# Attention scores on TensorE: the low parts of each head padded to 128 rows

## The chip, the core and the metric

The kernel runs on one core of one Trainium2 chip. A core has five engines that run side by side and meet at semaphores: TensorE (PE; its weight loads are listed apart as PEld), VectorE (DVE), ScalarE (ACT), GpSimd (POOL) and SyncE (SP, which here issues the transfers). The metric is the device time of one execution in microseconds (us), lower is better. A run is timed several times, and one execution is also recorded by the hardware profiler.

## The reference

One activation of 512 tokens by 1024 channels goes through two blocks of two layers each. Three of the mixers hold attention scores, and those are what the change touches:

```
# mLSTM, 8 heads of 64 (chunked in the reference):
s = einsum('bhtd,bhsd->bhts', qt, kt) * exp(dmat - m_t)
# causal attention with forget bias, 16 heads of 64:
logits = einsum('bqhd,bkhd->bhqk', qi, k) + (ci - c)
# neighbourhood attention, 8 heads of 64, plus 256 context keys:
s_loc = einsum('brqhd,brkwhd->bhrqkw', qg, k_band) * scale + bias
s_ctx = einsum('brqhd,bchd->bhrqc',  qg, k_ctx)  * scale
```

All inputs are float32, and every head has 64 dimensions, so a score product contracts over 64.

## The kernel before, in words

Features lie on the 128 partitions, tokens along the free dimension. To keep float32 accuracy with single-pass matmuls, each operand is split in two: a high part (the value rounded to the matmul format, written by ACT) and a low part (the rest, by DVE). A projection then takes three matmuls per block of 128 (`mm3`, L182 to L184, or L241 to L243 with the roles turned): high by high, high by low, low by high.

The kernel runs in eight stages, s0 to s7, one after another; names in the profile begin with the stage. s0 is the mLSTM mixer (`mlstm`), s2 the causal attention (`fox`), s4 the neighbourhood attention (`even_mixer`); s1, s3, s5 and s7 are feed-forward layers, s6 a convolution.

Scores are made for two heads at a time, since two heads of 64 fill the 128 partitions. `left` (L781) makes one tile per head: in the head's own 64 rows the high part, in the other 64 rows the low part. `right` (L787) makes three tiles: for each head a tile that holds the high part twice (L792 writes the copy, L799 the original), and a third tile that holds the low parts of both heads, each in its own 64 rows (DVE, L801). `dots` (L806) then makes the scores of both heads in two passes. The first pass (L809) runs over all 128 rows and sums high by high and low by high in one matmul. The second pass (L812) runs over the head's own 64 rows only, high by low. Per stage there are 32, 64 and 64 second-pass matmuls, 160 in all, with 128 to 512 columns.

`right` is called 18 times: 4 times in s0, 8 times in s2 (two pairs ahead of use), 6 times in s4 (4 pairs of heads, 2 tiles of context keys). Its tiles come from a pool of 53 slots that most tensors of the kernel share; a slot is handed on when its last reader is done.

Order: the program is written stage by stage, but a scheduler orders the instructions of each engine, and so places projection matmuls between those of the scores. Each engine then runs its own list strictly in that order. What stands around the change: in s2, POOL masks the diagonal blocks of the bias rows that DVE adds to the scores (L866, `affine_select`, four per head), in s0 it masks the decay tiles (L640), in s4 it takes square roots (L248). After the scores, DVE and ACT make the softmax (L878 to L891 in s2, L1116 to L1121 in s4), PE turns the probabilities over (L902, L1131) and multiplies by the values (L914, L1141, L1148). Score results lie in four PSUM banks ("aux").

Of the kernel before, what the change touches and what calls it, by code (L numbers as in the profile page):

```python
# [9 lines left out]
F32 = mybir.dt.float32  # L10
F32R = mybir.dt.float32r
AF = mybir.ActivationFunctionType
# [40 lines left out]
HALF = (slice(0, T // 2), slice(T // 2, T))  # L53
# [289 lines left out]
class Normed:  # L343
# [7 lines left out]
    def put(self, k, s, tmp=None):  # L351
        e = self.e
        self.tmp[k, s.start] = tmp
        if self.h[k] is None:
            self.h[k] = e.pair()
        hi, lo = self.h[k]
        return e.split(self.x[k][:, s], hi[:, s], lo[:, s], e.vec(self.w[0], self.w[1] + k))
# [216 lines left out]
def mlstm(e, A, x, first, pre, nxt, extra):  # L574
# [53 lines left out]
    def scores(j):  # L628
        a, b = left(e, kk[j]), right(e, q[j])
        both = e.triangles("dt")  # L630
        mbs = e.wide()
        for i in range(2):
            hd = 2 * j + i
            mb = mbs[:, i * T:(i + 1) * T]
            nc.sync.dma_start(out=mb, in_=md[hd:hd + 1, :].to_broadcast([P, T]))
            for sb in range(NT):
                d = both[i][sb]
                nc.scalar.activation(out=d, in_=mb[:, sb * P:], func=AF.Exp, scale=-1.0,
                                     bias=aT[:, sb * H + hd:sb * H + hd + 1])
                nc.gpsimd.affine_select(out=d[:, :P], in_=d[:, :P], pattern=[[1, P]], base=0, channel_multiplier=-1,  # L640
                                        compare_op=ALU.is_ge, fill=0.0)
        for sbs in ((0,), (1, 3), (2,)):
            ps = [e.bank("aux") for _ in range(2)]
            o = 0
            for sb in sbs:
                n = T - sb * P
                dots(e, [p[:, o:o + n] for p in ps], a, slice(sb * P, (sb + 1) * P), b, slice(sb * P, T))
                o += n
            for i in range(2):
                d = both[i][sbs[0]]  # L650
                if len(sbs) > 1:
                    d = both[i]["1,3"]
                nc.vector.tensor_tensor(out=d, in0=ps[i][:, :o], in1=d, op=ALU.mult)
        return both
# [116 lines left out]
ROWS2 = (slice(0, 64), slice(64, 128))  # L771
# [14 lines left out]

def right(e, t, scale=None, get=same, put=same, out=None):  # L787

    out = out or [e.slot(F32R, name="right") for _ in range(3)]
    for i, r in enumerate(ROWS2):  # L790
        a = out[i]
        e.nc.scalar.activation(out=put(a[ROWS2[1 - i]]), in_=get(t[r]), func=AF.Copy, scale=scale or 1.0)  # L792
        high_low(e, get(t[r]), put(a[r]), put(a[r].bitcast(F32)), put(out[2][r]), scale)
    return out


def high_low(e, src, hi, hi32, lo, scale):
    nc = e.nc
    nc.scalar.activation(out=hi, in_=src, func=AF.Copy, scale=scale or 1.0)  # L799
    if scale is None:  # L800
        nc.vector.tensor_tensor(out=lo, in0=src, in1=hi32, op=ALU.subtract)  # L801
    else:
        nc.vector.scalar_tensor_tensor(out=lo, in0=src, scalar=scale, in1=hi32, op0=ALU.mult, op1=ALU.subtract)


def dots(e, ps, a, acols, b, bcols):  # L806

    for i in range(2):
        e.nc.tensor.matmul(ps[i], lhsT=a[i][:, acols], rhs=b[i][:, bcols], start=True, stop=False)  # L809
    for i in range(2):  # L810
        r = ROWS2[i]
        e.nc.tensor.matmul(ps[i], lhsT=a[i][r, acols], rhs=b[2][r, bcols], start=False, stop=True)  # L812


def fox(e, A, x, wk, pre, nxt):
# [40 lines left out]
    def scores(j):  # L856
# [14 lines left out]
        for qt in range(NT):  # L871
            n = (qt + 1) * P
            ps = [e.bank("aux")[:, :n] for _ in range(2)]
            dots(e, ps, a, slice(qt * P, n), b, slice(0, n))
            for i in range(2):
                p = pr[i][3 - qt]
                m = e.small(5, "mx")
                nc.vector.tensor_tensor_reduce(out=p[:, qt * P:n], in0=ps[i][:, qt * P:n],  # L878
                                               in1=diag[i][:, qt * P:n], op0=ALU.add, op1=ALU.max, scale=1.0,
                                               scalar=NEG, accum_out=m[:, 0:1])  # L880
                if qt:
                    nc.vector.tensor_tensor_reduce(out=p[:, :qt * P], in0=ps[i][:, :qt * P],
                                                   in1=bias[i][:, :qt * P], op0=ALU.add, op1=ALU.max, scale=1.0,
                                                   scalar=NEG, accum_out=m[:, 1:2])
                    nc.vector.tensor_scalar(out=m[:, 2:3], in0=m[:, 0:1], scalar1=m[:, 1:2], scalar2=-1.0,
                                            op0=ALU.max, op1=ALU.mult)
                else:
                    nc.vector.tensor_scalar(out=m[:, 2:3], in0=m[:, 0:1], scalar1=-1.0, scalar2=None, op0=ALU.mult)
                nc.scalar.activation(out=p, in_=p, func=AF.Exp, bias=m[:, 2:3], accum_out=m[:, 3:4])
                nc.vector.reciprocal(m[:, 4:5], m[:, 3:4])  # L890
                nc.vector.tensor_scalar(out=p, in0=p, scalar1=m[:, 4:5], scalar2=None, op0=ALU.mult)  # L891
# [27 lines left out]
    raw, os = [], []  # L919
    queries(1)  # L920
    sides = {0: right(e, kk[0]), 1: right(e, kk[1])}
    pr, th = scores(0), gate()
    for j in range(KT):
        if j + 1 < KT:
            queries(1)
        after = (scores(j + 1), gate()) if j + 1 < KT else None
        if j + 2 < KT:
            sides[j + 2] = right(e, kk[j + 2])
        if j == KT - 2:
            os = [e.split_new(t, 0.5) for t in raw]  # L930
        raw.append(values(j, pr, th))
        if after:
            pr, th = after
        if os:
            os.append(e.split_new(raw[j], 0.5))
# [72 lines left out]
def even_mixer(e, A, x, first, pre, nxt):  # L1008
# [16 lines left out]
    kt, kc = [], []  # L1025
# [9 lines left out]
    for side, n in ((hc, 2), (h, NT)):  # L1035
        for j in range(n):
            t = e.slot(name="v")
# [6 lines left out]
    wqk = Weights(e, A["mix_w_qk"])  # L1044
    project(1)
    for t in kt:
        three = right(e, t)
        kc += [[c[:, s] for c in three] for s in HALF]
    v = {}
    for c in (0, 16, 8, 24, 40, 32, 48):  # L1050
        v[c] = e.slot(name="vw")
# [44 lines left out]
    def scores(j, half):  # L1096
        if half == 0:
            biases[j] = []
            for i in range(2):
                t = e.wide()  # L1100
                nc.sync.dma_start(out=t, in_=A["rpb"][2 * j + i])
                biases[j].append(t)
        pr = [[e.slot(name="p") for _ in range(2)] for _ in range(2)]
        for z in range(2):
            qt = half * 2 + z
            k0, which = WINDOWS[qt][0] * ROWS, (0, 1, 1, 2)[qt]
            ps = [e.bank("aux") for _ in range(2)]
            a, own = q[j], kk[j]
            for b, cols, d in ((own, slice(k0, k0 + 256), HALF[0]), (kc[j], HALF[0], HALF[1])):
                dots(e, [p[:, d] for p in ps], a, slice(qt * P, (qt + 1) * P), b, cols)  # L1110
            for i in range(2):
                p, b, s = pr[i][z], biases[j][i], e.small(4, "sm")
                b = bass.AP(tensor=b.tensor, offset=b[:, which * 256:].offset,
                            ap=[list(b.ap[0]), [768 - 256 * which, 2], [1, 256]])
                two = "p (a b) -> p a b"
                nc.vector.tensor_tensor_reduce(out=p.rearrange(two, a=2), in0=ps[i].rearrange(two, a=2), in1=b,  # L1116
                                               op0=ALU.add, op1=ALU.max, scale=1.0, scalar=NEG, accum_out=s[:, 0:1])
                nc.vector.tensor_scalar(out=s[:, 1:2], in0=s[:, 0:1], scalar1=-1.0, scalar2=None, op0=ALU.mult)
                nc.scalar.activation(out=p, in_=p, func=AF.Exp, bias=s[:, 1:2], accum_out=s[:, 2:3])
                nc.vector.reciprocal(s[:, 3:4], s[:, 2:3])  # L1120
                nc.vector.tensor_scalar(out=p, in0=p, scalar1=s[:, 3:4], scalar2=None, op0=ALU.mult)  # L1121
        return pr
# [29 lines left out]
    a, b, out = [], [], []  # L1152
    pr = scores(*steps[0])
    spatial_norm()
    for n, (j, half) in enumerate(steps):
# [6 lines left out]
        if n == len(steps) - 1:  # L1162
            out = [e.split_new(t) for t in a]
            out += [e.split_new(t) for t in b]
        values(j, half, pr, po)
        if half == 1:
            t = e.slot(name="b")
# [464 lines left out]
```

## Time and profile before

| | |
|---|---|
| median of 3 runs | 2566.67 us (2564.92 to 2566.76) |
| the profiled execution | 2563.47 us, of which span 2561.7 us |
| PE busy | 2496.2 us, 97% of the span |
| DVE busy | 1598.2 us, 62% |
| ACT busy | 1135.8 us, 44% |
| POOL busy | 76.7 us, 3% |
| mean granted TensorE clock | 0.988 |

Busy times add up how long an engine held instructions. For PE they are modelled ends of pipelined matmuls, so "97% busy" does not say that it ran at its peak: the distance from one matmul's start to the next one's start says how fast they follow each other. Where a row of the timeline merges several equal instructions (x2), its start is that of the first.

### The profile page before, as it was taken

How to read it: one execution, taken by the hardware profiler on the slowest of the kernel's cores; microseconds unless marked ns; L12 is line 12 of the kernel's file. 1: busy time of each engine (PE TensorE's matmuls, PEld its weight loads, DVE VectorE, ACT ScalarE, POOL GpSimd, SP SyncE). 2: the span in 40 equal slices, each digit the busy share in tenths (PEclk: the TensorE clock that was granted, in tenths of full speed). 3: DMA queues.
4: the chain of work that ended last, by engine and by line, in shares of the span. 5: the costliest groups of instructions: out<-in, count | busy, mean ns of one | idle time of the engine just before them, and what ended most of it. 6: DMA issues, size and time to landing. Idle time of an engine off the chain costs nothing.

```text
span 2561.7 us, 33896 instructions
## 1 busy us (share of the span) xinstructions
PE 2496.2 (97%) x12954; PEld 2043.8 (80%) x12954; DVE 1598.2 (62%) x3249; ACT 1135.8 (44%) x1882; POOL 76.7 (3%) x226
## 2 busy tenths in 40 slices
PE   9999999999999999999999999999999999999998
PEld 7778888888776688888887768878889678888887
DVE  7776866676557758576776665837375566634343
ACT  6555534243357645342445653423234765423231
POOL 0110000000001000000000000000000000000000
PEclk9999999999999999999999999999999998999999
DMA  6433243422332322424234223536251320322221
GB/s 214 173 113 124 94 145 110 140 91 76 120 107 83 109 77 99 157 98 164 91 114 134 101 85 112 184 130 237 103 210 64 103 81 32 101 91 99 91 91 34
DMA packets 91475, 293.27 MB, mean 114 GB/s; under 512 B 10008, under 2 KB 16408, under 8 KB 91312
## 3 DMA queue, kind: packets, MB, share of 16 engines
q1 hardware_dynamic: 90080, 290.04, 32.8%
q8 instruction: 102, 1.67, 0.3%
q10 hardware_dynamic: 1232, 1.06, 0.1%
q14 instruction: 61, 0.50, 0.1%
HBM read 283.67 MB, written 7.39 MB: 114 GB/s over the span
## 4 chain that ended last, share of the span: by engine, by line
PE 84%; ACT 5%; DVE 5%; issue 3%; DMA 1%; POOL 1%; POOLq 0%; SPq 0%; DVEq 0%; ACTq 0%
PE s1aux L184 3%; PE s1aux L182 3%; PE s1aux L183 3%; PE s3aux L182 3%; PE s3aux L184 3%; PE s3aux L183 3%; PE s7aux L182 2%; PE s7aux L184 2%; PE s7aux L183 2%; PE s5aux L183 2%; PE s5aux L184 2%; PE s5aux L182 2%; PE s1mm L184 2%; PE s1mm L182 2%; PE s1mm L183 2%
## 5 line engine op out<-in xcount | busy, mean ns | idle before, releaser
L170 DVE TENSOR_TENSOR s7wlo<-s7wst,s7whi 128x1024 fp32r<-128x1024 f32 x60 | 73.5, 1225 | 132.5 <-ACT s7whi L169 122.4
L169 ACT ACTIVATE s5whi<-s5wst 128x1024 fp32r<-128x1024 f32 x64 | 68.0, 1063 | 177.6 <-PE s5aux L183 85.8
L169 ACT ACTIVATE s7whi<-s7wst 128x1024 fp32r<-128x1024 f32 x60 | 63.7, 1062 | 168.0 <-PE s7aux L183 89.2
L170 DVE TENSOR_TENSOR s5wlo<-s5wst,s5whi 128x1024 fp32r<-128x1024 f32 x64 | 78.2, 1224 | 76.5 <-ACT s5whi L169 76.2
L169 ACT ACTIVATE s3whi<-s3wst 128x1024 fp32r<-128x1024 f32 x66 | 70.0, 1061 | 101.0 <-PE s3aux L183 53.6
L169 ACT ACTIVATE s1whi<-s1wst 128x1024 fp32r<-128x1024 f32 x66 | 69.8, 1061 | 97.6 <-PE s1aux L183 46.4
L170 DVE TENSOR_TENSOR s3wlo<-s3wst,s3whi 128x1024 fp32r<-128x1024 f32 x66 | 80.8, 1224 | 33.6 <-ACT s3whi L169 33.3
L170 DVE TENSOR_TENSOR s1wlo<-s1wst,s1whi 128x1024 fp32r<-128x1024 f32 x66 | 80.7, 1223 | 31.7 <-ACT s1whi L169 31.5
L170 DVE TENSOR_TENSOR s2wlo<-s2wst,s2whi 128x1024 fp32r<-128x1024 f32 (+1 forms) x41 | 49.2, 1200 | 57.6 <-ACT s2whi L169 57.4
L182 PE MATMUL s2mm<-s2hh,s2whi 128*128 128x512 f32 (+1 forms) x192 | 73.0, 386 | 2.5 <-ACT s2hh L169 1.3
L183 PE MATMUL s2mm<-s2hl,s2whi 128*128 128x512 f32 (+1 forms) x192 | 73.9, 386 | 0.0
L184 PE MATMUL s2mm<-s2hh,s2wlo 128*128 128x512 f32 (+1 forms) x192 | 73.8, 385 | 0.0
L184 PE MATMUL s1aux<-s0hh,s1wlo 128*128 128x512 f32 x176 | 69.8, 396 | 0.0
L182 PE MATMUL s3aux<-s2hh,s3whi 128*128 128x512 f32 x176 | 69.3, 394 | 0.0
L184 PE MATMUL s3aux<-s2hh,s3wlo 128*128 128x512 f32 x176 | 69.3, 394 | 0.0
L183 PE MATMUL s3aux<-s2hl,s3whi 128*128 128x512 f32 x176 | 69.3, 394 | 0.0
L183 PE MATMUL s1aux<-s0hl,s1whi 128*128 128x512 f32 x176 | 69.2, 393 | 0.0
L182 PE MATMUL s1aux<-s0hh,s1whi 128*128 128x512 f32 x176 | 69.2, 393 | 0.0
L752 DVE SCALAR_TENSOR_TENSOR s1c<-s1u,vecs,s1c 128x511 f32<-128x511 f32 (+1 forms) x88 | 65.2, 748 | 5.0 <-ACT s1c L750 3.6
L169 ACT ACTIVATE s2whi<-s2wst 128x1024 fp32r<-128x1024 f32 (+1 forms) x41 | 42.6, 1041 | 55.0 <-PE s2mm L183 40.4
L752 DVE SCALAR_TENSOR_TENSOR s3c<-s3u,vecs,s3c 128x511 f32<-128x511 f32 (+1 forms) x88 | 64.9, 747 | 2.8 <-ACT s3c L750 1.5
L970 DVE CUSTOM_DVE_ANT_0 s5mj<-s5wm,sc 128x512 f32<-128x512 f32 x96 | 62.4, 688 | 0.3
(732 smaller groups left out, 8077.9 us busy)
## 6 DMA issues: line engine op xcount, KB each, us to landing
s5wst<-w_ff SPq DMA_DIRECT2D x60, 512.0 KB, 3.7
s7wst<-w_ff SPq DMA_DIRECT2D x60, 512.0 KB, 3.2
s5wm<-w_mod SPq DMA_DIRECT2D x48, 512.0 KB, 3.9
s1wst<-ffn_w_up SPq DMA_DIRECT2D x40, 512.0 KB, 3.2
s3wst<-ffn_w_up SPq DMA_DIRECT2D x40, 512.0 KB, 3.2
s1wst<-ffn_w_down SPq DMA_DIRECT2D x22, 512.0 KB, 3.2
s3wst<-ffn_w_down SPq DMA_DIRECT2D x22, 512.0 KB, 3.2
s6wst<-w_pw SPq DMA_DIRECT2D x20, 512.0 KB, 3.3
```

Of the source, the lines that this page charges most:

```text
L169: nc.scalar.activation(out=hi, in_=src, func=AF.Copy)
L170: return nc.vector.tensor_tensor(out=lo, in0=src, in1=hi.bitcast(F32), op=ALU.subtract)
L182: mm(ps, lhsT=w[0], rhs=h[0], start=first, stop=False)
L183: mm(ps, lhsT=w[0], rhs=h[1], start=False, stop=False)
L184: self.last = mm(ps, lhsT=w[1], rhs=h[0], start=False, stop=last)
L752: nc.vector.scalar_tensor_tensor(out=c[:, t:], in0=u[:, :T - t], scalar=w[2 - t], in1=c[:, t:], op0=ALU.mult, op1=ALU.add)
L970: nc.vector.tensor_tensor_reduce(out=junk, in0=w[:, i * T:(i + 1) * T], in1=sc[i], op0=ALU.mult, op1=ALU.add, scale=1.0, scalar=0.0, accum ...
```

## The change

`right` makes four tiles in place of three. The low parts of the two heads lie in tiles of their own; in each, the other 64 rows are set to zero by a memset on POOL. The second pass then runs over all 128 rows: the head's high rows meet its low part, and its low rows meet zeros.

```
-    out = out or [e.slot(F32R, name="right") for _ in range(3)]
+    out = out or [e.slot(F32R, name="right") for _ in range(4)]
     for i, r in enumerate(ROWS2):
-        a = out[i]
-        e.nc.scalar.activation(out=put(a[ROWS2[1 - i]]), in_=get(t[r]), func=AF.Copy, scale=scale or 1.0)
-        high_low(e, get(t[r]), put(a[r]), put(a[r].bitcast(F32)), put(out[2][r]), scale)
+        a, b = out[i], out[2 + i]
+        rest = ROWS2[1 - i]
+        e.nc.gpsimd.memset(b[rest].bitcast(F32), 0.0)
+        e.nc.scalar.activation(out=put(a[rest]), in_=get(t[r]), func=AF.Copy, scale=scale or 1.0)
+        high_low(e, get(t[r]), put(a[r]), put(a[r].bitcast(F32)), put(b[r]), scale)
@@ def dots
     for i in range(2):
-        r = ROWS2[i]
-        e.nc.tensor.matmul(ps[i], lhsT=a[i][r, acols], rhs=b[2][r, bcols], start=False, stop=True)
+        e.nc.tensor.matmul(ps[i], lhsT=a[i][:, acols], rhs=b[2 + i][:, bcols], start=False, stop=True)
@@ def even_mixer
-        three = right(e, t)
-        kc += [[c[:, s] for c in three] for s in HALF]
+        four = right(e, t)
+        kc += [[c[:, s] for c in four] for s in HALF]
```

The first pass is L811 in the changed kernel, the second L813, the memset L793, the mask L867.

PE in s2, the scores of the second pair of heads; `s2aux` are the score banks, `s2right_6357` is the tile with both heads' low parts. Before:

```order
L809 MATMUL s2aux_6579<-s2right_6356,s2left_6540 128x128
L812 MATMUL s2aux_6579<-s2right_6357,s2left_6540 128x128
L809 MATMUL s2aux_6596<-s2right_6355,s2left_6539 128x256
L809 MATMUL s2aux_6597<-s2right_6356,s2left_6540 128x256
L812 MATMUL s2aux_6596<-s2right_6357,s2left_6539 128x256
L812 MATMUL s2aux_6597<-s2right_6357,s2left_6540 128x256
L809 MATMUL s2aux_6616<-s2right_6355,s2left_6539 128x384
L809 MATMUL s2aux_6617<-s2right_6356,s2left_6540 128x384
L812 MATMUL s2aux_6616<-s2right_6357,s2left_6539 128x384
L812 MATMUL s2aux_6617<-s2right_6357,s2left_6540 128x384
```

And now, the same place:

```order
L811 MATMUL s2aux_6597<-s2right_6371,s2left_6558 128x128
L813 MATMUL s2aux_6597<-s2right_6373,s2left_6558 128x128
L811 MATMUL s2aux_6614<-s2right_6370,s2left_6557 128x256
L811 MATMUL s2aux_6615<-s2right_6371,s2left_6558 128x256
L813 MATMUL s2aux_6614<-s2right_6372,s2left_6557 128x256
L813 MATMUL s2aux_6615<-s2right_6373,s2left_6558 128x256
L811 MATMUL s2aux_6634<-s2right_6370,s2left_6557 128x384
L811 MATMUL s2aux_6635<-s2right_6371,s2left_6558 128x384
L813 MATMUL s2aux_6634<-s2right_6372,s2left_6557 128x384
L813 MATMUL s2aux_6635<-s2right_6373,s2left_6558 128x384
```

The order is the same; only the second pass reads a tile of each head's own (6372 and 6373 in place of 6357 twice).

PE in s0, the first scores, where `s0mm` are projection matmuls between them. Before:

```order
L809 MATMUL s0aux_974<-s0right_941,s0left_935 128x512
L183 MATMUL s0mm_1010<-hl_143,s0whi_1006 128x512
L184 MATMUL s0mm_1010<-hh_142,s0wlo_1007 128x512
L182 MATMUL s0mm_1010<-hh_146,s0whi_1006 128x512
L183 MATMUL s0mm_1010<-hl_147,s0whi_1006 128x512
L184 MATMUL s0mm_1010<-hh_146,s0wlo_1007 128x512
L812 MATMUL s0aux_974<-s0right_943,s0left_935 128x512
L182 MATMUL s0mm_1176<-hh_118,s0whi_1172 128x512
L809 MATMUL s0aux_975<-s0right_942,s0left_936 128x512
```

And now:

```order
L811 MATMUL s0aux_977<-s0right_941,s0left_935 128x512
L183 MATMUL s0mm_1182<-hl_143,s0whi_1178 128x512
L184 MATMUL s0mm_1182<-hh_142,s0wlo_1179 128x512
L811 MATMUL s0aux_978<-s0right_942,s0left_936 128x512
L811 MATMUL s0aux_985<-s0right_941,s0left_935 128x384
L811 MATMUL s0aux_986<-s0right_942,s0left_936 128x384
L813 MATMUL s0aux_977<-s0right_943,s0left_935 128x512
L813 MATMUL s0aux_985<-s0right_943,s0left_935 128x384
L811 MATMUL s0aux_985<-s0right_941,s0left_935 128x128
L813 MATMUL s0aux_978<-s0right_944,s0left_936 128x512
```

Four projection matmuls that stood between the first score matmuls now come after them.

POOL in s2, the masks of the bias rows (`s2wm`, one row of four masks per head). Before:

```order
L866 AFFINE_SELECT s2wm_6545<-s2wm_6545 128x128 x4
L866 AFFINE_SELECT s2wm_6559<-s2wm_6559 128x128 x4
L866 AFFINE_SELECT s2wm_6782<-s2wm_6782 128x128 x4
L866 AFFINE_SELECT s2wm_6796<-s2wm_6796 128x128 x4
L866 AFFINE_SELECT s2wm_7019<-s2wm_7019 128x128 x4
```

And now:

```order
L867 AFFINE_SELECT s2wm_6563<-s2wm_6563 128x128 x4
L793 MEMSET s2right_6360 64x512
L793 MEMSET s2right_6361 64x512
L793 MEMSET s2right_6372 64x512
L793 MEMSET s2right_6373 64x512
L867 AFFINE_SELECT s2wm_6577<-s2wm_6577 128x128 x4
L867 AFFINE_SELECT s2wm_6803<-s2wm_6803 128x128 x4
L793 MEMSET s2right_6709 64x512
L793 MEMSET s2right_6710 64x512
L867 AFFINE_SELECT s2wm_6817<-s2wm_6817 128x128 x4
```

From here to the end of the stage two memsets stand between the masks of one head of each pair and those of the other.

## Rows read from the trace of the kernel before

**Rows 1.** The page, share of the chain that ended last by engine.

```profile
PE 84%; ACT 5%; DVE 5%; issue 3%; DMA 1%; POOL 1%; POOLq 0%; SPq 0%; DVEq 0%; ACTq 0%
```

**Rows 2.** Stretches s0, s2, s4: length, then busy PE, PEld, DVE, ACT, POOL; clock; DMA.

```profile
86.00:172.00 86.00, 84.28 (x386) 63.81 (x386) 61.98 (x141) 53.71 (x121) 14.55 (x36) 0.97 0.38 129
740.00:885.00 145.00, 142.58 (x680) 99.02 (x679) 114.03 (x470) 96.44 (x217) 19.96 (x52) 1.00 0.25 82
1385.00:1535.00 150.00, 141.19 (x727) 105.69 (x726) 95.80 (x260) 90.47 (x137) 5.08 (x4) 0.95 0.28 92
```

**Rows 3.** Timeline of PE in s2: start, duration, line, output<-inputs, rows*columns of weights, shape.

```profile
759.53 0.22 PE L809 MATMUL s2aux<-s2right,s2left 128*128 128x128 f32 x1
759.68 0.33 PE L812 MATMUL s2aux<-s2right,s2left 64*128 64x128 f32 x1
...
760.27 0.40 PE L182 MATMUL s2mm<-s2hh,s2whi 128*128 128x512 f32 x1
760.50 0.39 PE L183 MATMUL s2mm<-s2hl,s2whi 128*128 128x512 f32 x1
...
764.52 0.39 PE L809 MATMUL s2aux<-s2right,s2left 128*128 128x512 f32 x1
764.84 0.50 PE L812 MATMUL s2aux<-s2right,s2left 64*128 64x512 f32 x1
765.27 0.50 PE L182 MATMUL s2mm<-s2hh,s2whi 128*128 128x512 f32 x1
765.61 0.39 PE L809 MATMUL s2aux<-s2right,s2left 128*128 128x512 f32 x1
```

**Rows 4.** Timeline of PE in s1, 256 columns, all over 128 rows.

```profile
616.55 0.28 PE L184 MATMUL s1aux<-s1gh,s1wlo 128*128 128x256 f32 x1
616.67 0.28 PE L182 MATMUL s1aux<-s1gh,s1whi 128*128 128x256 f32 x1
```

**Rows 5.** Timeline of PE in s4: four score groups; a low part alone.

```profile
1461.59 0.40 PE L809 MATMUL s4aux<-s4right,s4left 128*128 128x256 f32 x2
1461.91 0.38 PE L812 MATMUL s4aux<-s4right,s4left 64*128 64x256 f32 x2
...
1464.47 0.51 PE L182 MATMUL s4mm<-s3hh,s4whi 128*128 128x512 f32 x1
...
1475.02 0.38 PE L812 MATMUL s4aux<-s4right,s4left 64*128 64x256 f32 x1
```

**Rows 6.** Instructions of L812: durations in ns min/median/max, first and last start, shapes.

```profile
L812 PE MATMUL s2aux<-s2right,s2left x64: 323/409/502, 743.3 to 882.9; 64*128 64x128 f32 x16, 64*128 64x256 f32 x16, 64*128 64x384 f32 x16, 64*128 64x512 f32 x16
L812 PE MATMUL s4aux<-s4right,s4left x64: 276/382/579, 1387.9 to 1531.8; 64*128 64x256 f32 x64
L812 PE MATMUL s0aux<-s0right,s0left x32: 322/381/504, 94.1 to 170.6; 64*128 64x512 f32 x8, 64*128 64x384 f32 x8, 64*128 64x128 f32 x8, 64*128 64x256 f32 x8
```

**Rows 7.** Waits of DVE in s2: who waited for whom, total us, times, longest.

```profile
DVE s2mx L890 <- ACT s2p L889: 8.2, 10, 1.2
```

**Rows 8.** Waits of PE in s4.

```profile
PE s4aux L809 <- DVE s4pt L1134: 3.6, 2, 1.8
```

**Rows 9.** Two stretches behind scores in s0, columns as in Rows 2.

```profile
99.00:103.00 4.00, 4.00 (x11) 3.12 (x11) 2.75 (x4) 0.00 (x0) 0.00 (x0) 0.57 0.23 88
171.00:174.50 3.50, 3.50 (x15) 3.31 (x16) 2.09 (x4) 0.74 (x4) 0.00 (x0) 0.52 0.30 108
```

**Rows 10.** PE's extra semaphore waits at the first pass, ns min/median/max.

```profile
L809 PEldq EVENT_SEMAPHORE  x37: 51/51/51, 92.5 to 1511.2; - x37
```

**Rows 11.** Groups of POOL's memsets: busy us, mean ns, then idle before.

```profile
L1272 POOL MEMSET s6yp<- 128x8 f32 x8 | 0.8, 104 | 53.6 <-PE s6aux L1321 23.0 <-ACT s6yv L1298 16.2 <-PE s6mm L1321 10.6
masks.py:197 POOL MEMSET ident<- 128x128 f32 x1 | 0.2, 204 | 0.3 <-POOLq L1624 0.3
```

**Rows 12.** Timeline of POOL and DVE in s2: a pair's masks, their first use.

```profile
771.91 2.91 POOL L866 TENSOR_SCALAR_AFFINE_SELECT s2wm<-s2wm 128x128 f32<-128x128 f32 x8 [10.29 <-DMA s2wm<-cdram]
779.77 0.28 DVE L878 CUSTOM_DVE_ANT_0 s2p<-s2aux,s2wm 128x128 f32<-128x128 f32 x1
```

## The prediction

> **What bounds the kernel now.** I read the page first: PE holds 84% of the chain of work that ended last [rows 1], so a microsecond saved on PE counts unless another engine is close behind. The change touches three stretches, and the busy times by stretch show how close: in s0 PE is busy 84.28 of 86 us and DVE 61.98, in s2 142.58 of 145 and DVE 114.03, in s4 141.19 of 150 with DVE and ACT near 90 to 96 [rows 2]. So s0 and s2 are PE's, with DVE 31 us behind in s2, and in s4 PE stands still for 8.8 us.
>
> Then I read the timeline of PE, by starts, not by busy times. Two projection matmuls of 512 columns start 0.23 us apart (760.27 to 760.50) [rows 3], two of 256 columns 0.12 us [rows 4]. Around a second-pass matmul (64 of 128 rows) this is not so. The first pass that starts at 764.52 is followed by the second at 764.84: 0.32. That is followed by a projection at 765.27: 0.43. And that by the next at 765.61: 0.34 [rows 3]. The three steps take 1.09 us where 3 x 0.23 = 0.69 would do. The operands had long been there (nothing in these rows waits for a semaphore). So going from 128 rows to 64 and back costs about 0.09 + 0.20 + 0.11 = 0.39 us (rounded) beyond the streaming, and I call it one excursion.
>
> For 128 columns the same three steps run from 759.53 to 760.27, 0.74 us [rows 3]. The streaming is 0.23 for the 512-column one plus two of 128 columns, which I take at 0.11 each (estimate: between 0.06, half of the 0.12 for 256 columns, and the 0.15 from 759.53 to 759.68, which has the entry in it). That leaves 0.29.
>
> Where both heads' second passes follow each other, they run side by side: two of them last 0.38 us as one does [rows 5]. So a pair has one excursion less one streaming time: 0.39 - 0.12 = 0.27 at 256 columns. Check: from 1461.59 to 1464.47 there are sixteen matmuls of 256 columns in four such groups, 2.88 us against 16 x 0.12 = 1.92; with the 0.11 that falls on the projection behind it the excess is 1.07, or 0.27 per pair.
>
> **The change, part by part.** *PE.* All 160 second passes become like the first; the excursions go, and with them the running side by side. In the three stretches of [rows 6] I counted 111 excursions along PE's timeline: 66 of one second pass, 41 of two, 4 of three.
> - s2: 15 alone at 128 columns x 0.29 = 4.4; 17 alone at 256 or 512 x 0.39 = 6.6; 8 pairs at 256 x 0.27 = 2.2; 8 pairs at 384 x 0.21 (0.39 less 0.175, between 0.12 and 0.23) = 1.7. Sum 14.9.
> - s4: 18 alone x 0.39 = 7.0, 23 pairs x 0.27 = 6.2. Sum 13.2.
> - s0: 14 alone x 0.39, 2 at 128 columns x 0.29, 2 pairs of 128 columns at 0.28, and 4 threes at about 0.25 (one streaming time less). Sum 7.6.
>
> PE's own work shrinks by 35.7 us. What of it shortens the end is less, because other work comes up behind.
>
> In s2, DVE is busy 114.0 us and waits 8.2 for ACT's exponentials, which a faster PE does not shorten [rows 2, 7]: 122.2 of 145. There is room for 14.9, but in bursts DVE is already the later one; I take 11.5. In s4 PE waits for DVE to empty banks, 3.6 us in two places [rows 8], and what PE saves just ahead of such a place it waits there. The two clusters of four pairs ahead of them (the one from 1461 and its like one round later) I count as nothing: 13.2 - 2.2 = 11, and of this I take 9. In s0 fewer projection matmuls stand between the first scores than before, so PE meets DVE's low parts sooner and waits there; I take 5.5 of 7.6. Sum 26. The ends are 0 (everything waits for DVE and ACT instead) and 35.7.
>
> *The clock.* Behind two of the four score bursts in s0, the granted clock is 0.57 over 4 us and 0.52 over 3.5 us [rows 9], a mixture of the two levels, mostly the 1.2 GHz one; before each fall PE ran scores with gaps. Each costs (1 - 0.57) x 4 = 1.7 us and (1 - 0.52) x 3.5 = 1.7 us. Without gaps both may go; new waits in s4 may bring others. I count half, -1.7; ends -3.4 and +3.4.
>
> *Semaphores.* Each tile of low parts now has two writers, DVE and POOL. PE's extra wait instruction takes 51 ns where it exists [rows 10]; for 36 tiles that is 1.8 us, mostly beside a running matmul. Half: +0.9; ends 0 and 1.8.
>
> *POOL.* 36 memsets of 64 x 512 (8, 16, 12). No row shows this size. A memset of 8 columns takes 104 ns and one of 128 columns 204 [rows 11]; on that line 512 columns take 0.52 us, 19 us in all, on an engine that is busy 20 of 145 us in s2. Ends: 0.1 and 1 us each. The cover is POOL's idle time: a pair's masks end at 774.82 and DVE needs the first at 779.77, 4.9 us later [rows 12]. Queued behind a memset are the masks of one head, and for them wait DVE's L878, the softmax, and PE's transposes. Two memsets take 1.0 of the 4.9. So nothing, as long as the memset itself does not wait long for a free slot; see the rivals.
>
> *Slots.* Eighteen more tiles go through the 53 slots, three more living at once in s2. Their wait is the memset's wait. DVE and ACT do the same number of instructions of the same size.
>
> Sum: -26 - 1.7 + 0.9 = -27 against the profiled execution's 2563.5, so 2536.5. That execution lies 3.2 us under the median of the runs, 2566.7. In terms of the median: about 2540.
>
> **A rule against it.** The rows show that two second passes on different halves of the rows start together and last as one [rows 5]. The Trainium skill, TensorEngine Tiling (Array Packing), sections Theoretical Speedup and Key Properties, says that tiles of at most 64 rows work independently and can bring up to twofold speed; by that alone the change gives away parallel work. The same list says that a change of tiling mode drains the engine, and the 0.39 us agrees with that. By the first alone the sum would be +6 (rival 2), by both the -35.7 above.
>
> **The rivals.**
> 1. *DVE and ACT become the bound.* For: in s2 only 22.8 us lie between DVE's 122.2 and the stretch; in s4 PE already waits. Against: PE's list has projection matmuls to fill in, and PE waits only 2.4 us in s2. Then only a third of the 35.7 arrives: -12, 2555.
> 2. *The step is not the change of rows.* If the 0.39 belongs to the second write into the same bank, it stays, and only the running side by side is lost: 31 second halves at 0.12 (3.7), 8 at 0.175 (1.4), 0.8 in s0. That is +6: 2573, slower. Against: the entry of 0.09 falls before the second pass starts, and the 0.11 on a projection into another bank.
> 3. *Memsets hold up the masks.* Each memset needs its slot first, and POOL's list is strict. If in s2 the slot comes free only when the previous pair's last product is done, half of an 18 us round (145 / 8) late, the masks come 9 - 3.9 = 5.1 us after they are needed, for 7 pairs: +36, less 27, or 2576. It decides from a wait of 3.9 us on. Against: the memsets are for tiles that are used a pair later, and the score order in s2 hardly moved.
> 4. *No change*: PE's gain is eaten exactly, 2566.
>
> **How the numbers follow.** The forecast, 2527 to 2550 (a gain of 17 to 40), 0.66; a gain beyond 40, 0.03; rival 1 (2551 to 2561) 0.17; rival 2, 0.04; rival 3, 0.05; rival 4, 0.05. No change means within 0.2%, 5 us, about what runs of this kernel can tell. Faster 0.66 + 0.03 + 0.17 = 0.86, same 0.05, slower 0.09. The range of 8 in 10 reaches from 2525, all of PE's gain with the clock's, to 2558, most of rival 1.
>
> **What would show it.** In the profile after: second passes of 128 rows that start 0.12 or 0.23 us before the next matmul, and no 0.39 around them; s2 shorter by 9 to 14 us, s4 by 6 to 11, s0 by 4 to 8; memsets near 0.5 us; DVE's share in these stretches higher. Wrong would be: spacing still over 0.3 us around L813 with operands ready (rival 2); DVE's L878 waiting for POOL (rival 3); PE waiting for DVE by as much as the excursions took (rival 1).

## The result, and the profile after

The change makes the kernel faster: 2537.08 us as the median of four runs (2536.32 to 2539.84) against 2566.52 of four runs of before on the same chip, ratio 0.9889 [0.9871, 0.9906]. A second measurement of the changed kernel gave 0.988 [0.9862, 0.9898]. The forecast was 2540 with 2525 to 2558. The profiled execution after took 2536.32 us, of which span 2534.6, against 2563.47 and 2561.7 before.

I start again with the chain of work that ended last. Its share by engine after:

```profile
PE 81%; ACT 6%; DVE 6%; issue 5%; POOL 1%; DMA 1%; SPq 0%; POOLq 0%; DVEq 0%; ACTq 0%
```

PE had 84% [rows 1]. Over the whole kernel it still holds most of the chain, and ACT and DVE have come a percent each closer. Inside s2 far more has changed. The same chain by line there (the lines are cut off on the right), in the window 740 to 885 before, then in 735 to 874 after:

```profile
by line: PE s2mm L183 15.8%; PE s2mm L184 14.6%; PE s2mm L182 14.6%; PE s2aux L812 10.5%; PE s2st L914 9.5%; PE s2aux L809 8.5%; PE s2aux L902 6.6%; ACT s2right L792 4.1%; ACT s2right L799 3.9%; ACT s2p L889 3.9%; ACT s2whi L169 2.1%; issue
```

```profile
by line: ACT s2p L890 10.3%; issue 8.4%; PE s2st L915 8.3%; ACT s2right L794 6.3%; ACT s2whi L169 6.0%; ACT s2right L801 6.0%; PE s2mm L183 5.7%; PE s2aux L811 5.4%; PE s2mm L182 5.3%; PE s2mm L184 5.2%; DVE s2wlo L170 4.6%; PE s2aux L813 3
```

Summed by engine, the chain through s2 was 80% PE, 17% ACT and 1% DVE; now it is 37% PE, 35% ACT and 19% DVE. In s0 PE fell from 84% to 47% and ACT rose from 9% to 28%, in s4 the shares hardly moved (PE 62% and 58%). PE is still busy for 134.74 of 139 us in s2, which suggests that two paths of about the same length run there now, one of PE's matmuls and one over ACT and DVE. The three score stretches by windows of the changed kernel (columns as in [rows 2]; each window moved with its stage):

```profile
90.00:168.00 78.00, 74.98 (x384) 60.30 (x383) 58.73 (x138) 51.02 (x121) 17.86 (x42) 1.00 0.40 133
735.00:874.00 139.00, 134.74 (x690) 99.82 (x688) 113.16 (x468) 96.36 (x217) 26.44 (x64) 1.00 0.27 86
1372.00:1510.00 138.00, 127.41 (x727) 102.28 (x727) 96.14 (x260) 90.05 (x138) 7.10 (x10) 0.96 0.31 100
```

The windows hold nearly the same counts of instructions as those of [rows 2], in 8, 6 and 12 us less. DVE's busy time hardly moved (61.98, 114.03 and 95.80 before), so its share rose: in s2 from 114.03 of 145 (79%) to 113.16 of 139 (81%).

The mechanism shows in the starts on PE's timeline. This is s2 of the changed kernel:

```profile
757.02 0.47 PE L811 MATMUL s2aux<-s2right,s2left 128*128 128x512 f32 x1
757.33 0.40 PE L813 MATMUL s2aux<-s2right,s2left 128*128 128x512 f32 x1
757.56 0.40 PE L184 MATMUL s2mm<-s2hh,s2wlo 128*128 128x512 f32 x1
757.80 0.47 PE L811 MATMUL s2aux<-s2right,s2left 128*128 128x512 f32 x1
758.11 0.39 PE L813 MATMUL s2aux<-s2right,s2left 128*128 128x512 f32 x1
```

The second pass (L813) starts 0.31 us behind the first pass, and the next matmul follows after 0.23 (757.33 to 757.56), the next after 0.24. Before these steps were 0.32, 0.43, 0.34 [rows 3]. So the two steps out of the short pass are gone, while the step into it has kept its size here (0.31 again from 757.80 to 758.11); below it turns out to have another cause. In s4, the four groups that answer to [rows 5]:

```profile
1443.01 0.40 PE L811 MATMUL s4aux<-s4right,s4left 128*128 128x256 f32 x2
1443.25 0.40 PE L813 MATMUL s4aux<-s4right,s4left 128*128 128x256 f32 x2
...
1444.68 0.40 PE L813 MATMUL s4aux<-s4right,s4left 128*128 128x256 f32 x2
1444.91 0.40 PE L182 MATMUL s4mm<-s3hh,s4whi 128*128 128x512 f32 x1
```

Sixteen matmuls of 256 columns take 1.90 us (1443.01 to 1444.91), 0.12 each, where they took 2.88. No step is longer than the streaming.

To see where the time came from I took, from each trace, the distance from the last matmul of one stage to the last of the next:

| | s0 | s1 | s2 | s3 | s4 | s5 | s6 | s7 | us at the low clock |
|---|---|---|---|---|---|---|---|---|---|
| before | 276.5 | 381.6 | 313.4 | 386.3 | 246.6 | 363.4 | 231.8 | 355.0 | 59.5 |
| after | 268.6 | 383.4 | 305.3 | 386.9 | 235.1 | 361.2 | 231.9 | 354.9 | 49.1 |
| difference | -7.9 | +1.8 | -8.1 | +0.6 | -11.5 | -2.2 | +0.1 | -0.1 | -10.4 |

The sum is -27.3 us, all of it in the three score stages but for -2.2 and +1.8 at their neighbours. Those two are mostly the clock. Behind bursts of scores and near some borders of stages the granted clock falls from 2.4 to 1.2 GHz for a few us. First the windows of before at such places, with 634 to 639 for comparison (columns as in [rows 2], the clock is the last number but two), then the windows of the kernel after, where 1577 to 1584 holds the border of s4 and s5:

```profile
634.00:639.00 5.00, 4.55 (x38) 4.35 (x38) 4.27 (x11) 0.39 (x1) 0.81 (x1) 1.00 0.49 159
1435.00:1441.00 6.00, 4.41 (x16) 3.59 (x17) 5.70 (x19) 5.94 (x12) 0.00 (x0) 0.72 0.53 193
1476.00:1482.00 6.00, 6.00 (x33) 4.11 (x31) 3.77 (x8) 3.20 (x5) 0.00 (x0) 0.72 0.27 99
1510.00:1518.00 8.00, 6.39 (x21) 3.61 (x23) 5.22 (x11) 5.75 (x8) 0.00 (x0) 0.65 0.49 173
1604.00:1609.00 5.00, 5.00 (x26) 4.72 (x27) 3.96 (x10) 2.77 (x7) 0.00 (x0) 0.66 0.00 0
```

```profile
99.00:103.00 4.00, 4.00 (x19) 3.26 (x18) 1.66 (x2) 0.10 (x1) 0.00 (x0) 1.00 0.59 159
165.00:169.00 4.00, 3.59 (x29) 3.50 (x30) 3.72 (x9) 1.74 (x6) 0.36 (x2) 1.00 0.75 266
634.00:639.00 5.00, 4.04 (x21) 4.04 (x22) 4.53 (x13) 2.82 (x8) 0.87 (x1) 0.66 0.46 177
1418.00:1424.00 6.00, 3.54 (x16) 3.06 (x17) 4.95 (x16) 5.94 (x11) 0.00 (x0) 0.72 0.36 122
1456.00:1462.00 6.00, 5.30 (x33) 3.95 (x34) 4.20 (x8) 4.87 (x8) 0.00 (x0) 0.72 0.35 111
1490.00:1496.00 6.00, 4.29 (x16) 2.42 (x18) 4.97 (x10) 4.05 (x7) 0.00 (x0) 0.72 0.56 179
1577.00:1584.00 7.00, 5.82 (x43) 5.24 (x44) 4.25 (x13) 2.80 (x7) 0.69 (x1) 1.00 0.00 1
```

The two falls in s0 [rows 9] are gone, and with them 3.4 us; of the three in s4 the last was twice as long (1510 to 1518) and is now as the others (at most -1.7); one at the border of s4 and s5 is gone (-1.7); a new one stands in s1 (634 to 639, +1.7). Over the whole execution the time at the low clock falls from 59.5 to 49.1 us; at half speed that is worth at most 5.2 us. So of the 27 us at most some 5 are the clock, and some 22 are PE's work.

The other runs say the same. Each has its span and its mean granted clock, and time less span x (1 - clock) is an estimate of its time at the full clock; the clock has three decimals, so one run is good to 1.3 us. Its median is 2531.7 to 2532.9 in the three later sets of runs of before and 2510.4 in both sets of the change: 22 us. Executions of one kernel differ for this reason too: 21 runs of before have clocks of 0.985 to 0.990 and spread over 12 us.

### The profile page after: what moved, and what is told of

Read it like the earlier page. It is cut to its first block, busy times and chain, and to the rows that moved or that the text cites. A ratio compares the mean times of both kernels' runs of the same rounds, so it can differ in the third digit from the quotient of the medians.

```text
span 2534.6 us, 33988 instructions
## 1 busy us (share of the span) xinstructions
PE 2463.1 (97%) x12954; PEld 2037.2 (80%) x12954; DVE 1598.5 (63%) x3249; ACT 1134.3 (45%) x1882; POOL 94.8 (4%) x262
## 4 chain that ended last, share of the span: by engine, by line
PE 81%; ACT 6%; DVE 6%; issue 5%; POOL 1%; DMA 1%; SPq 0%; POOLq 0%; DVEq 0%; ACTq 0%
PE s1aux L184 3%; PE s1aux L182 3%; PE s1aux L183 3%; PE s3aux L184 3%; PE s3aux L182 3%; PE s3aux L183 3%; PE s5aux L182 3%; PE s5aux L183 3%; PE s5aux L184 3%; PE s7aux L183 2%; PE s7aux L184 2%; PE s7aux L182 2%; PE s7mm L183 2%; PE s1mm L184 2%; PE s7mm L182 2%
## 5 line engine op out<-in xcount | busy, mean ns | idle before, releaser
L170 DVE TENSOR_TENSOR s3wlo<-s3wst,s3whi 128x1024 fp32r<-128x1024 f32 x66 | 80.7, 1224 | 31.8 <-ACT s3whi L169 30.2
L184 PE MATMUL s3aux<-s2hh,s3wlo 128*128 128x512 f32 x192 | 75.5, 393 | 0.0
L182 PE MATMUL s3aux<-s2hh,s3whi 128*128 128x512 f32 x192 | 75.5, 393 | 0.0
L183 PE MATMUL s3aux<-s2hl,s3whi 128*128 128x512 f32 x192 | 75.3, 392 | 0.0
L184 PE MATMUL s2mm<-s2hh,s2wlo 128*128 128x512 f32 (+1 forms) x192 | 72.7, 379 | 0.0
L184 PE MATMUL s1aux<-s0hh,s1wlo 128*128 128x512 f32 x176 | 69.4, 394 | 0.0
```

Of the source, the lines that this page charges most:

```text
L170: return nc.vector.tensor_tensor(out=lo, in0=src, in1=hi.bitcast(F32), op=ALU.subtract)
L182: mm(ps, lhsT=w[0], rhs=h[0], start=first, stop=False)
L183: mm(ps, lhsT=w[0], rhs=h[1], start=False, stop=False)
L184: self.last = mm(ps, lhsT=w[1], rhs=h[0], start=False, stop=last)
```

## The experiments

Changes in a stage are given against the table above. All kernels are the changed one with the edit shown, unless the text says otherwise. The expectations speak of theories: A is that the change of rows costs 0.39 us per excursion, B that DVE holds s2 up, D that PE's waits at the first passes do; each has its numbers.

**Is it the second pass's rows, or what comes with them?** The tiles, memsets and waits stay, only the second pass goes back to 64 rows:

```
-        matmul(ps[i], lhsT=a[i][:, acols], rhs=b[2 + i][:, bcols], ...)
+        r = ROWS2[i]
+        matmul(ps[i], lhsT=a[i][r, acols], rhs=b[2 + i][r, bcols], ...)
```

> The changed kernel with one part undone: four tiles and the 36 memsets stay, but the second pass goes over 64 rows again. Theory A (the gain is the change of rows between matmuls, some 0.39 us each time): all of it is lost, the time is that of before or a little more, 2564 to 2572 us, and the starts around the second pass are 0.32, 0.43 and 0.34 us apart again. Rival (the gain is the new order, or that each head has a low tile of its own): the time stays near 2537.

Measured: 2561.6 us, ratio 0.9981 [0.997, 0.9993] to before. The gain is lost but for 3.5 us, and its stages show next to none in the scores (s0 277.0, s2 314.1, s4 245.3, against 276.5, 313.4 and 246.6). The old spacing is back, as its timeline in s2 shows:

```profile
766.61 0.39 PE L811 MATMUL s2aux<-s2right,s2left 128*128 128x512 f32 x1
766.92 0.50 PE L814 MATMUL s2aux<-s2right,s2left 64*128 64x512 f32 x1
767.36 0.50 PE L184 MATMUL s2mm<-s2hh,s2wlo 128*128 128x512 f32 x1
767.69 0.40 PE L811 MATMUL s2aux<-s2right,s2left 128*128 128x512 f32 x1
```

0.31, 0.44, 0.33: the excursion as in [rows 3] (L814 is the second pass here). The rows of the second pass alone are worth 0.9889 / 0.9981 = 0.991, or 24 us; the new tiles, memsets and waits cost nothing that shows. The 3.5 us come from the clock: its ten runs have a median granted clock of 0.989, the 21 of before 0.987, and at the full clock, by the estimate above, it is no faster than before, 2534.2 against 2532.3.

This kernel is the best comparison of all, since its matmuls in s0, s2 and s4 start in the order of the changed kernel (4310 of 4312 stand in the same place), while those of before do not. In s2 neither kernel has a stretch at the low clock, in s4 both have 10.2 us: 314.1 became 305.3 (8.8 us) and 245.3 became 235.1 (10.2 us) by the rows alone. The chain through s2 still has 78% PE, 17% ACT and 1% DVE here; it is the rows that brought ACT and DVE onto it.

**One stage at a time.** `right` makes the three old tiles in all stages but one, and `dots` chooses by their number:

```
+    if out is None and e.stage != "s0":     # "s2", "s4" in the other two
+        out = [e.slot(F32R, name="right") for _ in range(3)]
...
+        if len(b) == 4:
```

> The 128-row second pass in s0 alone, the other stages as before. Theory A with stages that add up: 7 to 9 us faster than before (2558 to 2560), of which about 3 come from the two stretches at the lower clock behind the scores. If the clock stretches are chance, 4 to 5 us (2562).

> The 128-row second pass in s2 alone. If the stages add up as the two traces show: 6 to 7 us faster than before (2560). The term in the prediction was 11.5 us (2555). If s2 gains only through what s0 left behind: 0 to 3 us.

> The 128-row second pass in s4 alone. If the stages add up: 11 to 14 us faster than before, with the 2 us that s5 gained through the clock (2553 to 2556). The term in the prediction was 9 us (2557.5).

Measured, against 2565.09 of before: s0 alone 2558.57, 0.9968 [0.9957, 0.9979]; s2 alone 2559.28, 0.9976 [0.9963, 0.9989]; s4 alone 2547.42, 0.9925 [0.9911, 0.994]. In its own stage each kernel is within 1.3 us of the whole change: s0 269.9 (268.6), s2 306.5 (305.3), s4 234.3 (235.1). The medians add up to -30 (6.5 + 5.8 + 17.7), the change itself gave -29. The third kernel came out 6 us under what was expected of it, the first two as expected. What differs are places where the clock falls: with s4 alone 47.5 us of the execution are at the low clock, with s0 alone 75.0 (before 59.5), and not only in the stage that was edited. At the full clock, by the estimate above, the three give 6.1, 4.5 and 9.7 us, 20 in all, where the whole change gives 22.

**Is 0.39 us the price of the rows anywhere?** In the feed-forward stages s5 and s7 there are no score tiles, next to no POOL work, and no change of bank next to the matmuls in question. There I split the low matmul of one (s5) or two (s7) weight blocks per full tile and issue only its first 64 rows:

```
+            if n == T and k in {"s5": (3,), "s7": (2, 5)}.get(self.stage, ()):
+                rows = ROWS2[:1]
...
+        for r in rows or (slice(0, P),):
+            mm(ps, lhsT=w[0][r], rhs=h[1][r], start=False, stop=False)
```

> The changed kernel, and away from the scores: in the feed-forward layers s5 and s7, one (s5) or two (s7) of the matmuls of each full tile of 512 columns contract over 64 of 128 rows; the other half of that low part is left out. No tile, wait or bank is new. 49 places in s5, 98 in s7. Theory A (0.39 us per change of rows and back, anywhere): s5 19 us longer, s7 38 us longer, 2590 to 2597 us. Rival (the cost belongs to the second write into a score bank): nothing, 2537.

Measured: 2595.02 us against 2563.69, ratio 1.0122 [1.0105, 1.0139]. s5 grew from 361.2 to 380.7 with 49 such matmuls, 0.398 us each; s7 from 354.9 to 393.2 with 98, 0.391 each. Its timeline in s5 (L184 is the low matmul):

```profile
1599.93 0.39 PE L182 MATMUL s5mm<-s4hh,s5whi 128*128 128x512 f32 x1
1600.24 0.50 PE L184 MATMUL s5mm<-s4hl,s5whi 64*128 64x512 f32 x1
1600.68 0.50 PE L185 MATMUL s5mm<-s4hh,s5wlo 128*128 128x512 f32 x1
1601.02 0.39 PE L182 MATMUL s5mm<-s4hh,s5whi 128*128 128x512 f32 x1
1601.25 0.39 PE L184 MATMUL s5mm<-s4hl,s5whi 128*128 128x512 f32 x1
```

0.31, 0.44, 0.34, then 0.23 where all are 128 rows. Every one of the 147 places takes 1.07 to 1.10 us for its three steps, where three of 0.23 make 0.69. The matmuls of such a group all write one bank, those of 64 rows and those of 128 alike, so the step does not come from a second write into the same bank (rival 2 of the prediction) but from the rows. Half the work in the matmul, and it costs 0.39 us more.

**What keeps s2 from gaining its 14.9 us?** s2 gave 8.1. The theory of a bound by DVE: with less work on DVE the change should bring more. I left the division of the softmax out in s2, from before and from after:

```
-                nc.vector.reciprocal(m[:, 4:5], m[:, 3:4])
-                nc.vector.tensor_scalar(out=p, in0=p, scalar1=m[:, 4:5], ...)
```

> The kernel before, with the softmax's division left out in s2 (64 reciprocals and 64 scalings on DVE, some 33 us of DVE's 114 in that stage). To be compared with the next run. If DVE bounds s2 before already, s2 gets shorter by several us; if PE does, by 0 to 2 us.

> The changed kernel with the same division left out in s2. Theory B (in s2 PE's saving of 15 us was more than halved because DVE came up behind): with a light DVE the change saves 10 to 15 us in s2, and the difference to the previous run is 31 to 36 us. Rival (what is left of the 15 us is lost in PE's own list): s2 gains 6.5 us as with the full DVE, and the difference is 27.

Measured: on before 2570.72, 1.0025 [1.0014, 1.0036], so slower; on after 2534.39, 0.9883 [0.9865, 0.9902]. Their windows over s2, the first of before without the division, the second of after without it:

```profile
742.00:889.00 147.00, 143.87 (x678) 99.65 (x676) 88.37 (x340) 94.53 (x213) 16.14 (x52) 1.00 0.25 81
```

```profile
736.00:872.00 136.00, 132.26 (x682) 99.44 (x681) 89.11 (x342) 94.65 (x214) 23.19 (x64) 1.00 0.28 88
```

DVE has 24 to 26 us less to do in both (88.37 and 89.11). The difference between the two kernels, 36.3 us, is what the theory of DVE's load asked for, but it does not bear the theory out. Much of it is the clock: the light kernel of before ran at a mean granted clock of 0.9865, the other at 0.9902, and at the full clock, by the estimate above, they are 25 us apart, against 22 with the division. And the light kernel of before became 5.1 us longer in s2 (318.5): its PE list is in another order there (1138 of 1624 matmuls stand in the same place), and 3.4 us of its s2 are at the low clock, which is worth at most 1.7. On the changed kernel the 24 us are worth 1.7 us (303.6 against 305.3), here too with another order (1099 of 1624). The chain through s2 goes back to 69% PE, 24% ACT and 1% DVE, so with less to do DVE does leave it, but little time comes of that. A bound by DVE's load alone is not borne out; with the order changed as well, it is not ruled out cleanly either. This pair shows what a comparison of two kernels is worth when the edit lets a scheduler choose again: little, unless the order of both is looked at.

**Moving the same work instead.** The scaling of the probabilities on POOL in place of DVE, in s2:

```
-                nc.vector.tensor_scalar(out=p, in0=p, scalar1=m[:, 4:5], ...)
+                nc.gpsimd.tensor_scalar(out=p, in0=p, scalar1=m[:, 4:5], ...)
```

> The changed kernel with the 64 scalings of s2 (L892, some 24 us) on POOL in place of DVE. Theory B: 3 to 8 us faster than the change, 2529 to 2534. Rival: POOL takes over 1 us for each and holds up the masks queued behind, no gain or slower, 2537 to 2550.

Measured: 2542.52, 0.9914 [0.9898, 0.993], 5 to 7 us behind the change. The line's instructions in this kernel, ns min/median/max:

```profile
L892 POOL TENSOR_SCALAR s2p<-s2p,s2mx x64: 605/1088/2372, 742.5 to 880.7; 128x128 f32<-128x128 f32 x16, 128x256 f32<-128x256 f32 x16, 128x384 f32<-128x384 f32 x16, 128x512 f32<-128x512 f32 x16
```

On DVE the same line takes 386 ns in the median (changed kernel), on POOL 1088. s2 takes 307.7 us, 2.4 more than with the change, though DVE is freed of these instructions.

**Queries earlier.** What is left of s2's waits sits at first passes, some behind DVE's low part of the queries (`left`). So the queries were projected two pairs ahead instead of one:

```
-    queries(1)
+    queries(2)
...
-        if j + 1 < KT:
+        if j + 2 < KT:
             queries(1)
```

> The changed kernel with the query projections of s2 one pair further ahead, so that the left-hand tiles are ready a round before their scores. Theory D (what is left in s2 are PE's waits at the first passes, 7.7 us over steady starts, mostly for left-hand tiles that come just in time): s2 3 to 6 us shorter, about 2531. Rival (they are waits for score banks, or the slots run short): s2 as long or longer, 2535 to 2545.

Measured: 2539.17, 0.989 [0.9872, 0.9907], and s2 306.3, 1.0 longer. By starts on PE's timeline, the time beyond steady spacing around the second passes and into the first ones fell by 1.1 us, but that at transposes grew. Waits of PE in s2, who waited for whom, total us, times, longest:

```profile
PE s2aux L903 <- ACT s2pt L909: 3.3, 6, 0.6
PE s2aux L811 <- DVE s2mx L879: 1.9, 4, 0.5
```

PE's transposes (L903) now wait 3.3 us for ACT, where they waited 1.6 in the changed kernel. Not confirmed: one wait was exchanged for another.

**One score bank more.** Five banks for scores and two for projections, in place of four and three. `ANY`, the order in which matmuls that may use either kind take their banks, had to follow:

```
-BANKS = {"mm": 3, "aux": 4, "st": 1}
-ANY = ("mm", "aux", "mm", "aux", "mm", "aux", "aux")
+BANKS = {"mm": 2, "aux": 5, "st": 1}
+ANY = ("aux", "mm", "aux", "aux", "mm", "aux", "aux")
```

> The changed kernel with five score banks and two projection banks in place of four and three, in all stages. If the waits left in s2 and s4 are for score banks (PE waits 2 x 2.8 us in s4, and at the transposes in s2): s2 and s4 together 5 to 10 us shorter, 2525 to 2530, unless two projection banks cost that elsewhere. Theory D: s2 hardly moves.

Measured: 2549.53, 0.9932 [0.9912, 0.9953], 14 us behind the change on the same chip (2535.74), so neither expectation came. Most of it is in s2: 317.0, +11.7; s0 267.4, s4 236.6. Its waits of PE in s2:

```profile
PE s2mm L182 <- ACT s2th L854: 2.9, 1, 2.9
PE s2aux L811 <- DVE s2left L805: 2.0, 1, 2.0
```

The projections, now with two banks, wait for ACT to empty one (2.9), and the scores for the low part of a query that is late for that reason (2.0). Besides, 6.8 us of s2 are at the low clock here (granted 0.57 from 747 to 755), where the changed kernel has none in s2; that is worth at most 3.4. Some 3 of the 11.7 us stay without a name.

No kernel was faster than the change beyond what its own repetition shows, and none took work off ACT.

## Why the prediction was right, and where not

**The price of an excursion: right.** 0.39 us was read from three steps in [rows 3]; 49 and 98 of them placed elsewhere measured 0.398 and 0.391. That two second passes side by side cost 0.27 at 256 columns is borne out by the four groups in s4: 2.88 us became 1.90, where the working gave 1.92. Over all three stages, the time beyond steady spacing (0.23, 0.175, 0.12 and 0.06 us by columns) at steps into, out of and just behind second passes is 42.3 us before, 43.1 in the kernel with unused zeros and 10.5 after: 31.8 us gone, where the working counted 35.7. The prediction weighed two statements of the Trainium skill, TensorEngine Tiling (Array Packing): Theoretical Speedup (up to twofold for at most 64 rows) and Key Properties (a change of tiling mode drains the engine). The 24 us between this change and the kernel with unused zeros are in line with the second, though no run shows a drain as such; the first does not pay here, where short passes, alone or two and three together, stand between matmuls of 128 rows.

**The spacing after: right, with a second cause at some places.** Where the first pass had its operands and bank in time, the two passes of 512 columns now follow each other at 0.23 us, in s2 too:

```profile
775.25 0.39 PE L811 MATMUL s2aux<-s2right,s2left 128*128 128x512 f32 x1
775.48 0.40 PE L813 MATMUL s2aux<-s2right,s2left 128*128 128x512 f32 x1
```

The 0.31 that were left at 757.02 and 757.80 would have spoken for rival 2. The timeline of DVE and of PE's weight loads at these two places gives another reason:

```profile
756.79 0.08 DVE L883 DVE_READ_ACCUMULATOR2_ANT s2mx<- 128x1 f32 x1
756.99 0.19 PEld L811 LDWEIGHTS s2aux<-s2right,s2left 128*128 128x128 f32 x1 [0.38 <-PE s2aux L813]
...
757.57 0.08 DVE L883 DVE_READ_ACCUMULATOR2_ANT s2mx<- 128x1 f32 x1
757.77 0.19 PEld L811 LDWEIGHTS s2aux<-s2right,s2left 128*128 128x128 f32 x1 [0.25 <-PE s2aux L813]
```

DVE ends its reading of a bank at 756.87 and at 757.65; both times the first pass's weight load starts 0.12 us later, and the matmul 0.03 behind that (757.02, 757.80), so the load is not hidden, and the first pass lasts 0.47 instead of 0.39. It is a late release, not a change of rows. All of s2 bears this out: of 48 first passes that a second one follows at once, 26 had their weight load start less than 0.06 us ahead of them, and these are 0.06 to 0.11 us over the steady step; the other 22 are at most 0.03 over. That the step into a short pass has a price of its own is seen in the feed-forward stages, where no DVE stands ahead and it is 0.31 (1599.93 to 1600.24).

**s2: the term that was too large.** Forecast 11.5 of 14.9, measured 8.1 with no change of clock inside. By starts on PE's timeline, the time beyond steady spacing around second passes fell from 17.1 to 5.6 us, so 11.5 of the 14.9 did go; but the steps into first passes grew from 1.4 to 3.9, and those of transposes and value products from 20.7 to 23.3. The step that failed is "in bursts DVE is already the later one; I take 11.5": 6.8 us were lost there, not 3.4, and the engine named was only half of it, since the chain through s2 went over to ACT (17% to 35%) as much as to DVE (1% to 19%). On ACT these are above all the exponentials (L890, 14.3 us of the chain) and the two copies of `right` (L794 and L801, 17.2). The time went into many short waits of the kind shown above; the wait list of the changed kernel in s2 names only the longer ones, here two of DVE's and one of PE's:

```profile
DVE s2mx L891 <- ACT s2p L890: 5.6, 12, 1.1
DVE s2th L917 <- PE s2st L915: 7.4, 4, 1.8
PE s2aux L811 <- DVE s2mx L883: 1.3, 1, 1.3
```

Which engine would have to be faster is not settled, as no run took work off ACT. Less work on DVE brought 1.7 us, earlier queries cost 1.0, a bank more cost 11.7 (at most 3.4 of it the clock), the scaling on POOL 2.4. All four also changed the order of PE's list.

**s4: right, a little small.** Forecast 9, with PE's waits for DVE's banks as the limit. Measured 11.5 in s4 and 2.2 in s5; two falls of the clock less (1.7 each, above) would be 3.4 of that, which leaves 10.3. The one in s4 may be worth less: a second execution of the changed kernel has 13.6 us at the low clock in s4, as many as before, and takes the same 235.1 us. Against the kernel with unused zeros, at equal low time, s4 gave 10.2. The two clusters that the prediction counted as nothing were lost as it said; the wait that [rows 8] show with 3.6 us is now

```profile
PE s4aux L811 <- DVE s4pt L1135: 5.0, 2, 2.5
```

1.4 us longer, in two places again, where the prediction counted 2.2 for the two clusters.

**s0 and the clock.** s0 gave 7.9: the forecast had 5.5 for the work, and in the clock's term half of the 3.4 of [rows 9]. Both falls went, so 4.5 are the work. The reason given holds: the excess around second passes in s0 fell by 6.6 us, and that at steps into first passes grew by 2.8. Over the whole kernel the clock's term was -1.7 with ends of -3.4 and +3.4; the trace has up to -5.2. It was mis-sized because only s0 was looked at: [rows 9] hold two falls, while the execution of before has 59.5 us at the low clock in more places, and two places (1605, 635) changed although no instruction there was edited. The experiments with one stage each show how far that goes, 47.5 to 75.0 us. That the sum came so close is partly luck: two errors, s2 too large by 3.4 and the clock too small by up to 3.5, cancel, and so nearly do s0 (1.0 too large) and s4 (1.2 too small). Of the ranges that the prediction gave for the stages, s2 (9 to 14) was missed by 0.9 and s4 (6 to 11) by 0.5.

**Memsets and semaphores: right.** The memsets of 64 x 512 in s2, ns min/median/max, first and last start (s0 and s4 have the same times):

```profile
L793 POOL MEMSET s2right<- x16: 517/519/522, 719.4 to 842.4; 64x512 f32 x16
```

0.52 us, as the line through [rows 11] gave. They do wait for their slots as rival 3 said, and the next rows show how little comes of it among the scores of s2:

```profile
POOL s2right L793 <- PE s2st L915: 3.9, 6, 0.9
POOL s2right L793 <- ACT s2pt L909: 1.0, 1, 1.0
DVE s2p L879 <- POOL s2right L793: 0.2, 1, 0.2
```

The longest such wait is 1.0 us, where rival 3 would have decided from 3.9 on; DVE waited 0.2 us for POOL in all. Ahead of the scores of s2 four memsets wait 46.0 us together, and in s4 two wait 27.0 and 24.7, but no other engine waits for them there. PE's extra semaphore waits are now

```profile
L811 PEldq EVENT_SEMAPHORE  x38: 51/51/51, 92.7 to 1491.6; - x38
L813 PEldq EVENT_SEMAPHORE  x14: 51/51/51, 94.1 to 1380.0; - x14
```

52 where there were 37 [rows 10], so 15 more at 51 ns: 0.8 us where 0.9 was counted, and mostly beside a running matmul.

**The rivals.** Rival 2 (second write into a bank) falls by the fifth experiment, rival 3 by the rows above. Rival 1 (DVE and ACT become the bound) holds in part: s2 got 8.1 of 14.9, where it said a third, and the chain through s2 now runs for more than half over ACT and DVE (54%, before 18%). The light kernel speaks against DVE's load alone; what ACT's part is worth was not tried.

## What to carry to other kernels

A matmul over 64 rows between matmuls over 128 rows cost 0.39 us more here, at 512 columns and the full clock, than a matmul over all 128 rows, so where PE is the bound, count the changes of rows along its timeline by starts, and pad. The runs here hold short passes alone, in pairs and in threes; whether a long row of them, side by side, would win over padding was not tried. And a price that is read from starts holds on PE's own path, while the share that reaches the end has to be taken stage by stage, with the list of waits and the chain of that stage beside it: the chain of the whole kernel hid here that ACT had come up in s2. Where two kernels differ by a per cent, their granted clocks belong beside their times.

## What the runs showed of the hardware that was not expected

- The price of a change of rows is the same to 0.01 us in stages with nothing in common: 0.39 read around scores, 0.398 and 0.391 measured with 49 and 98 added in the feed-forward stages (by starts alone, medians of 0.40 and 0.39).
- The granted clock's low stretches last a few us each and move when code far from them changes: 45.7 to 75.0 us in all among the profiled kernels, whose matmul work is the same to within a per cent, so up to 14.6 us of elapsed time, at half speed, can come or go. That is half of what this change gains. They differ between executions of one kernel too: 49.1 and 52.5 us in two of the changed one.
- POOL scales a tile of 128 partitions by 128 columns in 606 ns and by 512 columns in 1565 (medians), DVE in 282 and 485.
- The matmul behind one whose weight load starts less than 0.06 us ahead of it comes late: in s2, 26 first passes of this kind are 0.06 to 0.11 us over the steady step to the second.
